# Order of an mLSTM head's products: the first output gate tile goes between the keys and the values

## The chip, the cores and the metric

The kernel runs on one core of a Trainium2 chip. Its metric is the device time of one execution in microseconds, the median of several runs. A core has TensorE (PE, matrix products into PSUM banks), VectorE (DVE), ScalarE (ACT), GpSimd (POOL) and SyncE (SP), which issues most of the DMAs. Each engine takes its instructions in order and waits for the others by semaphores.

## What is computed

Two layers of an encoder on one sequence of 512 tokens with 1024 channels, all in fp32. The sub-layer around the change is the mixer, and of it the bidirectional mLSTM branch with 4 heads of 256 channels. Cut to what matters:

```python
z = u @ w_in
qk_m, v_m, o_m, gate_m, qkv_a, gates_br = split(z)
def mlstm_branch(qk, v, o_pre, gate_pre, ...):
    qk = silu(centred_dwconv(qk, conv_w, conv_b))     # width 5
    q, k = split(qk); q = heads(q) * 256 ** -0.5
    h = mlstm_scan(q, k, v, i_f, f_f) + flip(mlstm_scan(flip(q), flip(k), flip(v), ...))
    hn = (h - mean(h)) * rsqrt(var(h) + eps)          # over a head's channels
    return sigmoid(o_pre) * hn * gn_w
# mlstm_scan: num = (q k^T * decay) v, den = its row sum, h = num / max(|den|, exp(-m))
```

## The kernel before

Every product of two fp32 matrices is done as three: each operand is split into a high half, rounded to fp32r (a cast on ACT, L87), and a low half, the rest (a subtraction on DVE, L88), and `mm3` issues high·high, low·high and high·low (L91 to L93). Weights come from HBM by SP's queue in loads of 1 MB into two raw buffers; each load is split in two parts into a ring of two pairs of high and low tiles, so the split of a third part waits until the products of the first have been done.

The mLSTM stage of a layer has for each head these blocks of products with the input u (8 slices of 128 channels), in `head_gemm`: two tiles each of queries and keys (`head_qk`, tiles `qk`, 24 products of 512 columns each); the values in two halves of 256 tokens (`head_v`, tiles `mv`, two of 128 tokens in each half, 48 products of 256 columns a half); two tiles of the output gate (`head_o`, tiles `o`, 24 products each). A half of the values goes over its first weights (`wvh`, `wvl`) for the first 12 products of a tile, and over the second from the 13th. A key tile is copied out of PSUM by ACT (`zp`, L1077), goes through the convolution (`cy`: L1079 on ACT, four L1081 on DVE), a tanh on ACT (L1082) and a product on DVE (L1083), and is split (`qkh`). A value tile is split out of PSUM (`vh` on ACT, L1105, `vl` on DVE, L1106). A gate tile goes through a tanh on ACT (`so`, L1114) and a scaling in place (L1116).

Then `head_scores` makes the weights `pt` of the numerator (it begins with `Amx`, L1144), and `head_out` does for each of four blocks of 128 tokens a numerator (`num`, 15 products a direction pair) and an output: `ht` is num over den (L1193 on ACT, L1194 on DVE), then its normalisation, its transposes on PE (`htp`, L1208) and its product with `so` (L1210, DVE).

What sets the order is `weave`: it takes one step of `head_gemm` for head h+1, then one step of `head_out` for head h. Each `yield` ends a step: a tile of queries, keys or gate, or a half of the values. The steps of `head_out` follow the table `HO`: numerators 0 and 1, output 0, numerator 2, output 1, numerator 3, outputs 2 and 3. Instructions of each engine stand in the order in which the code issues them, apart from small shifts by the builder (two numerator products, say, stand ahead of the block they belong to). Head 0's gate and queries are done elsewhere (`begun`), so a layer has three heads with the whole sequence.

PSUM tiles come in rings of two banks with a tag: "g" for queries, keys, gate tiles and the first half of the values; "A" for the second half of the values, numerators 1 and 3 and `Amx`; "n" for numerators 0 and 2; "S" for `htp` and the scores. A tile waits for the readers of the one that had its bank before.

Of the kernel before, what the change touches and what calls it, by code (L numbers as in the profile page):

```python
# [65 lines left out]
def encoder(ctx: ExitStack, tc: tile.TileContext, a, depth):  # L66
# [13 lines left out]
    def ps_tile(tag, name, shape=(P, T)):  # L80
        return psum.tile(list(shape), F32, tag=tag, name=name)
# [4 lines left out]
    def split(hi, lo, src, eng=None):  # L86
        S.copy(hi, src)  # L87
        (eng or V).tensor_tensor(lo, src, hi.bitcast(F32), op=ALU.subtract)  # L88

    def mm3(out, lh, ll, rh, rl, first, last):  # L90
        mm(out, lh, rh, start=first, stop=False)  # L91
        mm(out, lh, rl, start=False, stop=False)  # L92
        mm(out, ll, rh, start=False, stop=last)  # L93
# [24 lines left out]
    def w_feature(src, ktiles, name, own=None, count=2, eng=None):  # L118


        n = src.shape[1]
        cols = 2048 // ktiles
        srcv = src.rearrange("(k p) n -> p k n", p=P)
        for c0 in range(0, n, cols):
            cw = min(cols, n - c0)
            raw = raw_tile(name)
            rv = raw[:, :ktiles * cw].rearrange("p (k n) -> p k n", k=ktiles)
            Y.dma_start(rv, srcv[:, :, c0:c0 + cw])
            for j in range(cw // P):
                r = rv[:, :, j * P:(j + 1) * P]  # L130
                if own is not None and c0 // P + j < count:
                    yield split_own(r, ktiles, own, eng)
                    continue
                wh, wl = w_pair(name, 0, ktiles, P)
                split(wh, wl, r, G if name in POOL else V)
                yield [wh[:, k, :] for k in range(ktiles)], [wl[:, k, :] for k in range(ktiles)]
# [11 lines left out]
    def w_token(src, c0, cw, ktiles, name, own=None, own_k=(), early=False):  # L148

        srcv = src.rearrange("(k p) n -> p k n", p=P)  # L150
        per_raw = 2048 // cw
        per = 1024 // cw
        cuts = list(range(0, ktiles, per_raw)) + [ktiles]
        raws = []

        def load():
            i = len(raws)
            if i + 1 < len(cuts):
                k0, k1 = cuts[i], cuts[i + 1]
                raw = raw_tile(name)  # L160
                raws.append(raw[:, :(k1 - k0) * cw].rearrange("p (k n) -> p k n", n=cw))
                Y.dma_start(raws[i], srcv[:, k0:k1, c0:c0 + cw])

        if early:
            load()
        for i, (k0, k1) in enumerate(zip(cuts, cuts[1:])):
            load()
            rv = raws[i]
            for j in range(0, k1 - k0, per):
                m = min(per, k1 - k0 - j)  # L170
                if k0 + j in own_k:
                    for h in range(m):
                        wh, wl = own(), own()
                        split(wh[:], wl[:], rv[:, j + h, :])
                        yield wh[:], wl[:]
                else:
                    wh, wl = w_pair(name, SH if cw == 256 else 0, per, cw)
                    split(wh[:, :m], wl[:, :m], rv[:, j:j + m, :])
                    for h in range(m):
                        yield wh[:, h, :], wl[:, h, :]  # L180
# [554 lines left out]
    for l in range(depth):  # L735
# [13 lines left out]
        def slot(name, dt=F32):  # L749
            return X.tile([P, T], dt, tag="q", name=name, bufs=Q)  # L750
# [5 lines left out]
        def wk(name, shape=(P, T)):  # L756
            r = roles[name]
            return YP.tile(list(shape), F32, tag=r, name=name, bufs=depths[r])
# [303 lines left out]
        def product(w, name, fine):  # L1062

            if fine:
                return (yield from gemm_steps(w, uk, KT, name))
            return gemm_f(w, uk, KT, name)

        def head_qk(h, sec, out, fine=False):

            src = w_in[:, sec * COL_K + h * 256:sec * COL_K + h * 256 + 256]  # L1070
            for d, w in enumerate(w_feature(src, KT, "wqk")):
                n = sec * 8 + 2 * h + d
                ps = yield from product(w, "qk", fine)
                zp = wk("zp", (P, T + 4))
                G.memset(zp[:, 0:2], 0.0)
                G.memset(zp[:, T + 2:T + 4], 0.0)
                S.copy(zp[:, 2:T + 2], ps[:])  # L1077
                y = wk("cy")
                S.activation(y[:], zp[:, 0:T], AF.Identity, bias=vec["convb"](n), scale=vec["conv"](0, n))  # L1079
                for j in range(1, 5):  # L1080
                    V.scalar_tensor_tensor(y[:], zp[:, j:j + T], vec["conv"](j, n), y[:], op0=ALU.mult, op1=ALU.add)  # L1081
                S.activation(zp[:, 0:T], y[:], AF.Tanh, scale=0.5)  # L1082
                V.scalar_tensor_tensor(y[:], zp[:, 0:T], 1.0, y[:], op0=ALU.add, op1=ALU.mult)  # L1083
                th, tl = slot("qkh", F32R), slot("qkl", F32R)
                split(th[:], tl[:], y[:], G if n % 2 in GQ else V)
                out.append((th, tl))
                yield

        def head_v(h, out):
            vh = YP.tile([P, 4, NVP], F32R, tag="v", name="vh", bufs=VB)  # L1090
            vl = YP.tile([P, 4, NVP], F32R, tag="v", name="vl", bufs=VB)
            G.memset(vh[:, :, 256:257].bitcast(F32), 1.0)
            G.memset(vh[:, :, 257:258].bitcast(F32), 0.0)
            G.memset(vl[:, :, 256:258].bitcast(F32), 0.0)
            ws = list(w_token(w_in, COL_V + h * 256, 256, KT, "wv"))
            for i0 in (0, 2):
                pss = [ps_tile(MV[i0 // 2], "mv") for _ in range(2)]
                for k0 in (0, 4):
                    for i, ps in zip((i0, i0 + 1), pss):
                        for kk in range(k0, k0 + 4):  # L1100
                            uh, ul = uk[kk]
                            mm3(ps[:, 0:256], uh[:, i * P:(i + 1) * P], ul[:, i * P:(i + 1) * P],
                                ws[kk][0], ws[kk][1], kk == 0, kk == KT - 1)
                for i, ps in zip((i0, i0 + 1), pss):
                    S.copy(vh[:, i, 0:256], ps[:, 0:256])  # L1105
                    V.tensor_tensor(vl[:, i, 0:256], ps[:, 0:256], vh[:, i, 0:256].bitcast(F32), op=ALU.subtract)  # L1106
                yield
            out.extend((vh, vl))

        def head_o(h, out, fine=False):  # L1110
            so = X.tile([P, 2, T], F32, tag="hg", name=f"so{h}", bufs=4)
            for d, w in enumerate(w_feature(w_in[:, COL_O + h * 256:COL_O + h * 256 + 256], KT, "wo")):
                ps = yield from product(w, "o", fine)
                S.activation(so[:, d, :], ps[:], AF.Tanh, scale=0.5)  # L1114
                gn = vec["gnh"][:, 2 * h + d:2 * h + d + 1]
                S.activation(so[:, d, :], so[:, d, :], AF.Identity, bias=gn, scale=gn)  # L1116
                yield
            out.append(so)
# [8 lines left out]
        def head_gemm(h, out, begun=()):  # L1127

            so, qk = begun or ([], [])
            vs, o = [], [so]  # L1130
            if not begun:
                yield from head_qk(h, 0, qk)
            yield from head_qk(h, 1, qk)
            yield from head_v(h, vs)
            if not begun:
                o = []
                yield from head_o(h, o)
            out.extend((qk, *vs, o[0]))

        def head_scores(h, qk):  # L1140
# [89 lines left out]
        for _ in head_gemm(0, hd, lead):  # L1230
            pass
        for h in range(MH):
            qk, vh, vl, so = hd
            hgt.append(so)
            side = head_out(h, *head_scores(h, qk), vh, vl, so)
            if h < MH - 1:
                hd = []
                weave(head_gemm(h + 1, hd), side, *WV)
# [190 lines left out]
```

## Time and profile before

| | |
|---|---|
| median of 3 runs | 2280.37 us (2280.28 to 2283.35) |
| the profiled execution | 2288.52 us |
| its span, first to last instruction | 2286.7 us |
| PE busy | 2201.6 us, 96% of the span |
| PE's weight loads | 80% |
| DVE, ACT, POOL busy | 58%, 39%, 14% |
| mean granted PE clock | 0.985 |

All times of rows are from the profiled execution. A row of a timeline has the start in us from the span's start, the duration, the engine, the line of the kernel, the operation, output<-inputs and shapes; brackets at its end tell how long the engine idled before it and which instruction released it. PE's products overlap: the distance from one start to the next is what one of them costs.

### The profile page before, as it was taken

What the parts mean: (1) busy time and instruction counts of PE and PEld (TensorE: products, weight loads), DVE (VectorE), ACT (ScalarE), POOL (GpSimd) and SP (SyncE); (2) the same over time, 40 slices, a digit from 0 to 9 for tenths busy, and PEclk for the clock granted to TensorE, in tenths of its full rate; (3) what the DMA queues carried; (4) which work ended last, traced back from release to release, by engine and by line L of the source; (5) the groups of instructions that cost most, each with busy time, mean ns of one, the idle gap of its engine ahead of it and who ended that gap; (6) DMA issues with size and microseconds to landing.
All of it is one profiled execution on the core that took longest, in us unless ns stands there. A gap on an engine that the chain in (4) does not pass through costs nothing.

```text
span 2286.7 us, 30972 instructions
## 1 busy us (share of the span) xinstructions
PE 2201.6 (96%) x12353; PEld 1836.4 (80%) x12353; DVE 1315.9 (58%) x2242; ACT 884.0 (39%) x1465; POOL 321.6 (14%) x318
## 2 busy tenths in 40 slices
PE   6999999999999999999989999999999999999998
PEld 5878877878888878788878788788888879788886
DVE  8655458778554766564654544577764454633346
ACT  3544345544333522222354443455543324223222
POOL 4100013222000240000040000233300022200001
PEclk8999999999999999999999999999999999999999
DMA  8523322232343466554543223112212344423334
GB/s 239 186 83 107 101 66 97 74 111 80 111 157 113 155 206 205 189 193 167 189 152 98 61 92 107 56 62 69 74 56 92 111 157 157 152 83 102 100 112 157
DMA packets 244064, 278.79 MB, mean 122 GB/s; under 512 B 10280, under 2 KB 191184, under 8 KB 243920
## 3 DMA queue, kind: packets, MB, share of 16 engines
q1 hardware_dynamic: 238848, 258.97, 35.1%
q0 software_dynamic: 3584, 12.58, 1.6%
q10 hardware_dynamic: 1488, 5.26, 0.6%
q8 instruction: 97, 1.59, 0.3%
q14 instruction: 47, 0.39, 0.1%
HBM read 264.18 MB, written 12.60 MB: 121 GB/s over the span
## 4 chain that ended last, share of the span: by engine, by line
PE 75%; DVE 14%; ACT 3%; issue 3%; DMA 3%; POOL 2%; POOLq 0%; DVEq 0%; ACTq 0%; SPq 0%
PE z L93 6%; PE z L92 6%; PE z L91 6%; DVE cy L1081 4%; DMA aw<-in_w_ada 2%; PE aq L91 2%; PE ak L91 2%; PE f1y L92 2%; PE av L91 2%; PE f1y L91 2%; PE f1y L93 2%; PE av L93 2%; PE av L92 2%; PE aq L93 2%; PE aq L92 2%
## 5 line engine op out<-in xcount | busy, mean ns | idle before, releaser
L283 DVE SCALAR_TENSOR_TENSOR acc<-aw,cact,acc 128x512 f32<-128x512 f32 x140 | 118.3, 845 | 49.8 <-DMA aw<-in_w_ada 47.6
L1081 DVE SCALAR_TENSOR_TENSOR cy<-zp,vcols,cy 128x512 f32<-128x512 f32 x128 | 115.6, 903 | 10.4 <-ACT cy L1079 8.5
L87 ACT CAST w3h<-w 128x1024 fp32r<-128x1024 f32 x40 | 42.1, 1053 | 157.3 <-PE z L92 153.2
L88 POOL TENSOR_TENSOR wqkl<-wqk,wqkh 128x1024 fp32r<-128x1024 f32 x32 | 78.0, 2438 | 161.4 <-ACT wqkh L87 159.5
L978 ACT ACTIVATE xs<-xs,sm 128x512 f32<-128x512 f32 x64 | 46.2, 723 | 133.3 <-DVE sm L977 129.6
L87 ACT CAST w1h<-w 128x1024 fp32r<-128x1024 f32 x40 | 42.0, 1050 | 139.9 <-PE z L92 134.9
L88 DVE TENSOR_TENSOR w1l<-w,w1h 128x1024 fp32r<-128x1024 f32 x40 | 49.4, 1234 | 77.3 <-ACT w1h L87 77.3
L1337 DVE TENSOR_TENSOR sl<-sl,z 128x512 f32<-128x512 f32 x44 | 30.2, 687 | 104.9 <-PE z L93 101.2
L976 DVE CUSTOM_DVE_ANT_0 xs<-sc,bias 128x512 f32<-128x512 f32 x64 | 43.9, 691 | 74.7 <-PE sc L970 63.7
L91 PE MATMUL z<-um0h,w3h 128*128 128x512 f32 x160 | 64.2, 401 | 4.0 <-DVE sl L1337 4.0
L91 PE MATMUL z<-um1h,w3h 128*128 128x512 f32 x160 | 63.5, 397 | 1.8 <-DVE sl L1337 1.8
L93 PE MATMUL z<-um1h,w3l 128*128 128x512 f32 x160 | 63.6, 398 | 1.0 <-DVE w3l L88 1.0
L93 PE MATMUL z<-um0h,w3l 128*128 128x512 f32 x160 | 63.9, 400 | 0.5 <-DVE w3l L88 0.5
L92 PE MATMUL z<-um0l,w3h 128*128 128x512 f32 x160 | 63.8, 399 | 0.0
L92 PE MATMUL z<-um1l,w3h 128*128 128x512 f32 x160 | 63.2, 395 | 0.0
L91 PE MATMUL z<-um0h,w1h 128*128 128x512 f32 x160 | 63.1, 394 | 0.0
L93 PE MATMUL z<-um0h,w1l 128*128 128x512 f32 x160 | 62.7, 392 | 0.0
L92 PE MATMUL z<-um0l,w1h 128*128 128x512 f32 x160 | 62.5, 391 | 0.0
L91 PE MATMUL z<-um1h,w1h 128*128 128x512 f32 x160 | 62.4, 390 | 0.0
L93 PE MATMUL z<-um1h,w1l 128*128 128x512 f32 x160 | 62.3, 390 | 0.0
L92 PE MATMUL z<-um1l,w1h 128*128 128x512 f32 x160 | 62.2, 389 | 0.0
L935 POOL DMA_DIRECT2D vrow<-nat x16 | 11.8, 736 | 345.0 <-ACT nat L928 344.9
(544 smaller groups left out, 7268.0 us busy)
## 6 DMA issues: line engine op xcount, KB each, us to landing
w<-in_w SPq DMA_DIRECT2D x44, 1024.0 KB
aw<-in_w_ada SPq DMA_DIRECT2D x160, 256.0 KB
wqk<-in_w_in SPq DMA_DIRECT2D x16, 1024.0 KB
wav<-in_w_in SPq DMA_DIRECT2D x12, 1024.0 KB
wak<-in_w_in SPq DMA_DIRECT2D x20, 512.0 KB
f0v<-in_w SPq DMA_DIRECT2D x10, 1024.0 KB
f1v<-in_w SPq DMA_DIRECT2D x10, 1024.0 KB
waq<-in_w_in SPq DMA_DIRECT2D x18, 512.0 KB
```

The costliest lines, as they stand in the source:

```text
L87: S.copy(hi, src)
L88: (eng or V).tensor_tensor(lo, src, hi.bitcast(F32), op=ALU.subtract)
L91: mm(out, lh, rh, start=first, stop=False)
L92: mm(out, lh, rl, start=False, stop=False)
L93: mm(out, ll, rh, start=False, stop=last)
L283: V.scalar_tensor_tensor(acc[:], raws[k][:], c, acc[:], op0=ALU.mult, op1=ALU.add)
L935: G.dma_start(rows[i0 * P:(i0 + 2) * P, :].rearrange("(i p) c -> p i c", p=P), nat[:])
L976: V.tensor_tensor_reduce(x[:], sc[:], bias_tile(ti), 1.0, -3e38, ALU.add, ALU.max, sm[:, 0:1])
L978: S.activation(x[:], x[:], AF.Exp, bias=sm[:, 1:2], scale=ch, accum_out=sm[:, 2:3])
L1081: V.scalar_tensor_tensor(y[:], zp[:, j:j + T], vec["conv"](j, n), y[:], op0=ALU.mult, op1=ALU.add)
L1337: V.tensor_tensor(t[:], t[:], p3[:], op=ALU.mult)
```

## The change

In heads 1 to 3 the first tile of the output gate is now computed between the second tile of the keys and the first half of the values; the second gate tile stays behind the values. `head_o` becomes a generator that is advanced by one step there and run to its end later.

```diff
             vs, o = [], [so]
             if not begun:
+                o = []
+                outputs = head_o(h, o)
                 yield from head_qk(h, 0, qk)
             yield from head_qk(h, 1, qk)
+            if not begun:
+                yield next(outputs)
             yield from head_v(h, vs)
             if not begun:
-                o = []
-                yield from head_o(h, o)
+                yield from outputs
             out.extend((qk, *vs, o[0]))
```

With the table of steps, the products of head h+1 (left) and the steps of head h (right, num and out) alternate as follows. Before: q0 num0, q1 num1, k0 out0, k1 num2, v0 out1, v1 num3, o0 out2, o1 out3. After: q0 num0, q1 num1, k0 out0, k1 num2, **o0** out1, v0 num3, v1 out2, o1 out3. Lines behind the change are three higher in the kernel after (L1193 becomes L1196, L1208 becomes L1211); L1114 and L1116 are not.

ACT in head 1 of layer 0, before, from the second key tile's L1079 (zp_3897, cy_3901) on; mv are the four value tiles, wo the raw gate weights:

```order
L1079 ACTIVATE cy_3901<-zp_3897,vcols_688 128x512 [waits Activation_49,Pool_49]
L87 CAST qkh_3857<-cy_3849 128x512 [waits DVE_49]
L1193 ACTIVATE ht_3938<-num_3913,dn_3930 128x256 [waits DVE_49,PE_49]
L1082 ACTIVATE zp_3897<-cy_3901 128x512 [waits DVE_49,Activation_49]
L1105 CAST vh_3947<-mv_3962 128x256 [waits PE_49]
L87 CAST qkh_3909<-cy_3901 128x512 [waits DVE_49]
L1105 CAST vh_3947<-mv_3963 128x256 [waits PE_49]
L87 CAST woh_4111<-wo_4109 128x1024 [waits DMAHW7_49,PE_49]
L1105 CAST vh_3947<-mv_4020 128x256 [waits PE_49]
L1105 CAST vh_3947<-mv_4021 128x256 [waits PE_49]
```

ACT at the same place after (wvh_3997 is the cast of the values' second weights, so1 the gate):

```order
L1079 ACTIVATE cy_3901<-zp_3897,vcols_688 128x512 [waits Activation_49,Pool_49]
L87 CAST qkh_3857<-cy_3849 128x512 [waits DVE_49]
L1196 ACTIVATE ht_3938<-num_3913,dn_3930 128x256 [waits DVE_49,PE_49]
L1082 ACTIVATE zp_3897<-cy_3901 128x512 [waits DVE_49,Activation_49]
L87 CAST wvh_3997<-wv_3991 128x1024 [waits PE_49]
L87 CAST qkh_3909<-cy_3901 128x512 [waits DVE_49]
L1114 ACTIVATE so1_3947<-o_3954 128x512 [waits PE_49]
L1116 ACTIVATE so1_3947<-so1_3947,gnh_696 128x512 [waits Activation_49]
L1105 CAST vh_3986<-mv_4001 128x256 [waits PE_49]
L1105 CAST vh_3986<-mv_4002 128x256 [waits PE_49]
L1196 ACTIVATE ht_4080<-num_4055,dn_4072 128x256 [waits DVE_49,PE_49]
```

The casts of the gate weights (woh) left this stretch, since o0 has been computed by then; in their place the second cast of the value weights and the tanh and scaling of o0 stand behind L1082 of the second key tile.

PE in the first half of the values, before, at the second tile (mv_3963): the first weights are wvh_3954, and the wait is for ACT.

```order
L93 MATMUL mv_3962<-wvh_3954,u0l_105 128x256
L91 MATMUL mv_3962<-wvh_3954,u0h_104 128x256
L92 MATMUL mv_3962<-wvl_3955,u0h_104 128x256
L93 MATMUL mv_3962<-wvh_3954,u0l_105 128x256
L91 MATMUL mv_3963<-wvh_3954,u0h_104 128x256 [waits Activation_49]
L92 MATMUL mv_3963<-wvl_3955,u0h_104 128x256
```

PE in the first half of the values after (first weights wvh_3993, second wvh_3997; num_4055 is numerator 3 of head 0):

```order
L91 MATMUL mv_4001<-wvh_3993,u0h_104 128x256
L92 MATMUL mv_4001<-wvl_3994,u0h_104 128x256
L93 MATMUL mv_4001<-wvh_3993,u0l_105 128x256
L91 MATMUL mv_4001<-wvh_3997,u0h_104 128x256 [waits Activation_49]
L91 MATMUL num_4055<-vh_3436,pt_3567 128x258 [waits PE_49]
L92 MATMUL num_4055<-vl_3437,pt_3567 128x258
L91 MATMUL mv_4002<-wvh_3993,u0h_104 128x256 [waits Activation_49]
L92 MATMUL mv_4002<-wvl_3994,u0h_104 128x256
```

The 13th product of the first value tile, over the second weights, now waits for ACT, and the second value tile (mv_4002) waits for ACT behind it; two numerator products stand between them.

PE after, at the end of that numerator and the start of the second half of the values (mv_4089):

```order
L93 MATMUL num_4055<-vh_3436,pt_3568 128x258
L91 MATMUL num_4056<-vh_3436,pt_3569 128x258 [waits PE_49]
L92 MATMUL num_4056<-vl_3437,pt_3569 128x258
L93 MATMUL num_4056<-vh_3436,pt_3570 128x258
L1211 MATMUL htp_4143<-ident_66,ht_3938 128x128 [waits PE_49]
L1211 MATMUL htp_4143<-ident_66,ht_3938 128x128
L91 MATMUL mv_4089<-wvh_3993,u0h_104 128x256 [waits Activation_49]
L92 MATMUL mv_4089<-wvl_3994,u0h_104 128x256
```

The numerator now stands ahead of the second half of the values, whose first tile waits for ACT; before, that half stood ahead of the numerator.

## Rows read from the trace of the kernel before

**Rows 1.** The page: span, busy time of the engines, chain by engine.

```profile
span 2286.7 us, 30972 instructions
...
PE 2201.6 (96%) x12353; PEld 1836.4 (80%) x12353; DVE 1315.9 (58%) x2242; ACT 884.0 (39%) x1465; POOL 321.6 (14%) x318
...
PE 75%; DVE 14%; ACT 3%; issue 3%; DMA 3%; POOL 2%; POOLq 0%; DVEq 0%; ACTq 0%; SPq 0%
```

**Rows 2.** Timeline of PE, head 1 of layer 0 (start us, duration, ...).

```profile
409.80 0.28 PE L91 MATMUL mv<-wvh,u0h 128*128 128x256 f32 x1
...
412.76 0.38 PE L91 MATMUL mv<-wvh,u0h 128*128 128x256 f32 x1 [1.39 <-ACT zp L1077]
...
417.11 0.36 PE L91 MATMUL mv<-wvh,u0h 128*128 128x256 f32 x1
...
423.50 0.39 PE L91 MATMUL num<-vh,pt 128*128 128x258 f32 x1 [0.50 <-DVE vl L1106]
...
425.41 0.39 PE L91 MATMUL o<-u0h,woh 128*128 128x512 f32 x1
...
430.88 0.38 PE L1208 MATMUL htp<-ident,ht 128*128 128x128 f32 x2
...
436.73 0.71 PE L1144 MATMUL Amx<-mhl,sel 128*128 128x512 f32 x2
```

**Rows 3.** Timeline of PE, layer 1: last head's values, two Amx.

```profile
1625.90 0.71 PE L1144 MATMUL Amx<-mhl,sel 128*128 128x512 f32 x2
...
1662.64 0.38 PE L91 MATMUL mv<-wvh,uf0h 128*128 128x256 f32 x1 [1.37 <-ACT zp L1077]
...
1686.62 0.72 PE L1144 MATMUL Amx<-mhl,sel 128*128 128x512 f32 x2
```

**Rows 4.** Timeline of ACT, head 1 of layer 0.

```profile
417.78 0.64 ACT L1082 ACTIVATE zp<-cy 128x512 f32<-128x512 f32 x1 [0.23 <-DVE cy L1081]
...
418.32 0.35 ACT L1105 CAST vh<-mv 128x256 fp32r<-128x256 f32 x1
...
419.18 0.62 ACT L87 CAST qkh<-cy 128x512 fp32r<-128x512 f32 x1 [0.50 <-DVE cy L1083]
...
423.31 1.05 ACT L87 CAST woh<-wo 128x1024 fp32r<-128x1024 f32 x1
...
426.45 0.48 ACT L1193 ACTIVATE ht<-num,dn 128x256 f32<-128x256 f32 x1 [2.08 <-DVE dn L1191]
```

**Rows 5.** Timeline of DVE, head 1 of layer 0: convolution of the second keys.

```profile
413.65 0.75 DVE L1081 SCALAR_TENSOR_TENSOR cy<-zp,vcols,cy 128x512 f32<-128x512 f32 x1 [0.27 <-ACT cy L1079]
```

**Rows 6.** The gate tiles: xcount: min/median/max ns, first to last start.

```profile
L1114 ACT ACTIVATE so<-o x16: 576/592/595, 317.8 to 1687.0; 128x512 f32<-128x512 f32 x16
```

**Rows 7.** Timeline of PE, head 2 of layer 0.

```profile
478.30 0.38 PE L92 MATMUL mv<-wvl,u0h 128*128 128x256 f32 x1 [2.95 <-DVE wvl L88]
...
488.85 0.39 PE L91 MATMUL num<-vh,pt 128*128 128x258 f32 x1 [1.89 <-DVE vl L1106]
...
491.03 0.63 PE L91 MATMUL o<-u0h,woh 128*128 128x512 f32 x1
...
497.80 0.38 PE L1208 MATMUL htp<-ident,ht 128*128 128x128 f32 x2
```

**Rows 8.** PE by windows (us, busy, granted clock, DMA, GB/s), and a row of PE's timeline.

```profile
413.00:414.00 1.00, 1.00 (x10) 1.00 0.28 52
...
480.00:481.00 1.00, 1.00 (x11) 1.00 1.05 361
...
491.00:492.00 1.00, 1.00 (x5) 0.50 0.48 115
...
366.42 0.39 PE L92 MATMUL mv<-wvl,u0h 128*128 128x256 f32 x1 [2.66 <-DVE wvl L88]
```

**Rows 9.** Timelines of SP's queue and ACT: a load and its reader.

```profile
2262.20 0.37 SPq L162 DMA_DIRECT2D f1v<-in_w  x1
...
2267.23 1.05 ACT L87 CAST f1vh<-f1v 128x1024 fp32r<-128x1024 f32 x1 [2.56 <-DMA f1v<-in_w]
```

## The prediction

> **What bounds the kernel now.** I read the page's busy shares first. TensorE (PE) is busy for 2201.6 of 2286.7 us, VectorE (DVE) for 58%, and 75% of the chain that ended last is PE's [rows 1]. So a new order can give back only moments in which PE idles, and it costs what it adds to them. The change touches heads 1 to 3 of each layer's mLSTM stage, six places. Next I read PE's timeline through one of them, head 1 of layer 0 [rows 2]. The reader is to see two idle moments in brackets: 1.39 us at 412.76, where the 13th value product needs the PSUM bank that ScalarE's (ACT) copy of the second key tile (zp, L1077) frees, and 0.50 us at 423.50, where the numerator needs the low halves of the values (vl, L1106). The rest of these 27 us runs back to back. Five of the six heads show this pair, first [rows 2] and last [rows 3]; head 2 of layer 0 waits 2.95 and 1.89 us instead [rows 7].
>
> So the two existing waits, 1.89 us in a head, are all that the change can take away there. In the new order the first goes: the first gate tile (o0) now stands between the keys and the values, and runs over the copy. The second goes too, since a whole block of values lies between a vl and its reader.
>
> **The change part by part.** *Work.* Nothing is added or removed: the same products, casts and copies in another order, so the cost is the difference in idle time. I walk the new order of PE and ACT with the durations of before, from the same start, 409.80, since all up to there stands in the old order.
>
> o0 is 24 products, 425.41 to 430.88, 5.47 us, and a pair of transposes (htp) takes 0.13 [rows 2]. The values then start at 409.80 + 5.47 + 0.13 = 415.40. A block of 48 value products takes 423.50 − 0.50 − 417.11 = 5.89 us, 0.123 each, so the first 12 are through at 416.87.
>
> *First new wait.* The 13th reads the second half of the cast value weights (wvh). Its slot is that of o0's second weights, so the cast can't start before o0's end, 415.27; before, those weights were already there. On ACT it stands behind L1082 of the second key tile. That one started at 417.78, after DVE's L1081, and ACT went on at 418.32 [rows 4]. This is DVE's chain of the convolution, which began at 413.65 [rows 5]; nothing in the change stands before it, so I leave its times. A cast of this size takes 1.05 us [rows 4]: 418.32 + 1.05 = 419.37, and PE idles 419.37 − 416.87 = 2.50 us. Queued behind the waiting product on PE are two numerator products and all of the values; ACT's later casts of values wait for PE in turn. Bounds: 2.3 if ACT passes its queue a little sooner, 2.9 with a hop of some tenths at each hand-over, as the 0.23 and 0.50 of [rows 4].
>
> *Second new wait.* After the 13th and two numerator products (0.37 together) PE is at 419.74. The second value tile takes o0's PSUM bank, which the tanh (L1114) must read first. On ACT that stands behind the key's cast (qkh), 0.62 us [rows 4], starting near 419.27, then 0.59 of its own [rows 6]: 420.38, each starting 0.1 before the printed end of its neighbour, as 418.32 does. Idle: 0.64. Bounds 0.4 and 1.0.
>
> *Third new wait.* 35 value products (4.30) and 13 of the numerator (at 1.91/15 = 0.127: 1.65) end at 426.33; the transposes follow to 426.46. The second half of the values takes the banks of that numerator, which were free before it ran in the old order. Their reader is ACT's ht (L1193), then DVE. Before, the numerator ended at 425.41 and ht at 426.45 + 0.48 = 426.93, 1.52 us later [rows 2, 4]. So the next block starts at 427.85, idle 1.39. DVE's part frees the second bank within the 1.47 us of 12 products. Bounds 0.9 and 1.6.
>
> *Behind it.* The second block (48 products), o1 and the next head's scores follow as before, and o1's tanh has as much room as the old one had. Sum: 2.50 + 0.64 + 1.39 − 1.89 = +2.64 us in a head, 2.3 + 0.4 + 0.9 − 1.89 = 1.7 to 2.9 + 1.0 + 1.6 − 1.89 = 3.6 by the bounds.
>
> *Head 2 of layer 0.* Its key chain on DVE is mixed with other work, and its waits are 4.84 already [rows 7], so the new ones partly fall on the old ones. Bounds 0 and 2.64; I take the middle, 1.3. Five heads at 2.64 and this one: 14.5 us; by the bounds 8.5 to 20.6.
>
> *Loads.* The raw value weights are split some 9 us later, and the next queries' load takes over their buffer from SyncE's (SP) queue; the keys' load does so with the gate weights, some 8 us later. A load of 1 MB went from issue at 2262.20 to its first reader at 2267.23, 5.03 us [rows 9]; the next head reads its queries over 10 us after that buffer is free. I cost it at nothing: the values and o1 cover it. If this cover were gone, the price is at most those 5 us a head. The last head's gate weights are followed by another load in the same way, at most 0.5 us in each layer, which I leave out of the sum.
>
> *Clock.* PE's granted clock stood at 1.00 behind the 1.39 wait, at full 2.4 GHz (413 to 414), and at 0.50, 1.2 GHz, from 491 on, behind the 1.89 wait [rows 8]. Waits of 2.66 and 2.95 lie in this stage too [rows 7, 8]; the latter was not followed at once by a fall, at 480 the clock was 1.00 [rows 8]. What a fall costs: o0 started at 491.03 and ended at 497.80, 6.77 against 5.47, 1.3 more [rows 2, 7]; the numerator ahead of it took 491.03 − 488.85 = 2.18 against 1.91, 0.3 more. I take 1.5 us. The new first wait, 2.50, is nearest to the 1.89 and the 2.66 and not to the 1.39, and two more waits follow in ten microseconds, so I charge one fall to each of the five heads: 7.5 us. Head 2 has its fall already. Bounds: none, or a second fall in each.
>
> *Sum.* 14.5 + 7.5 = +22.0 us. The profiled execution took 2288.52 us (span 2286.7), which would be 2310.5; the median of the runs is 8.15 lower, 2280.37. The same 22.0 on it gives 2302.4.
>
> **The rivals.** *A, the clock stays.* PE waits as worked out, but the low clock comes in none of the five heads. For it: 2.95 with no fall at once. Against it: 1.89 and 2.66 with one. Time: +14.5, 2294.9, with the bounds 2289 to 2301.
>
> *B, faster.* The copy of the second key is covered by o0, and nothing takes its place: ACT would have to cast wvh before PE wants it at 416.87, and do the tanh before the second value tile. Then the old pairs go, 5 × 1.89 = 9.5, and up to 4.84 in head 2: 2266, or, where the third new wait stays (1.39 in a head), 5 × 0.50 and up to 3.4: 2274. It is decided on ACT by the place of wvh behind L1082: if the first two new waits together stay under 1.89 − 1.39 = 0.50 us, a head is no slower than before. The 417.78 of [rows 4] speaks against it, nearly a microsecond too late before the cast even starts. The Trainium skill, in "Perfetto Trace Analysis", section "Optimizing Tensor Performance", says that independent groups of products should rotate through PSUM banks so that ACT and DVE empty one while the next is computed; by that rule alone the change is a gain, as in this rival, for it parts the keys from the values by a group in another bank. The trace agrees on the bank that is freed, but the new waits are on a weight slot and on banks of other tiles.
>
> *C, no change.* The new waits come to the old sum, 1.9 in a head. With the third at 1.39 the first two must shrink from 3.14 to 0.50, so the convolution on DVE would have to end 2.6 us sooner; its time is 2276 to 2285.
>
> *D, still slower.* A second fall in each head, or a load that isn't hidden: another 7.5 to 10, 2310 to 2313.
>
> **How the numbers follow.** Forecast (waits and one fall in most heads): 0.60. A: 0.21. D: 0.07. B: 0.06. C: 0.06. The predicted time is 2302. The range takes the forecast's and A's bounds, from 2289 (8.5 us of waits) to 2312 (22.0 plus a size error or second falls in some heads of nearly 10); it leaves out B, C and some of D. A difference under 0.2%, 4.6 us, is about what a measurement can't tell from no change. Slower by more than that: 0.60 + 0.21 + 0.07 = 0.88; within it 0.06; faster 0.06.
>
> **What the profile after would show.** In each of the six heads: no wait on zp L1077 or vl L1106; a wait of about 2.5 on ACT's cast of wvh at the 13th value product, 0.6 on the tanh of so, and 1.4 on ACT's ht ahead of the second half of the values. From one Amx to the next in layer 1, 1686.62 − 1625.90 = 60.72 now [rows 3], I expect 63.4 without a fall of the clock and 64.9 with one, and some three slices of a microsecond near 0.50 behind the first wait. Wrong would be: the first wait below 1 us (ACT came to the cast sooner, rival B or C), no low clock (A), a wait on a load (D), or a stretch of DVE's convolution that moved, since every anchor of the first two waits is its end.

## The result, and the profile after

The changed kernel takes 2307.9 us (median of four runs, 2302.68 to 2308.87). The kernel before takes 2280.32 over its four runs beside it, and 2281.52 and 2281.28 over the 11 and the 23 runs beside the experiments. The ratio is 1.0114, with an interval from 1.0098 to 1.013. That is some 26 us more (22 to 30 by the interval), where 22 were forecast; 2307.9 lies in the range.

The page of the profile after shows little of this, as the change adds no work; the lines answer to [rows 1]:

```profile
span 2307.0 us, 30959 instructions
...
PE 2206.7 (96%) x12353; PEld 1840.4 (80%) x12353; DVE 1319.4 (57%) x2242; ACT 883.1 (38%) x1465; POOL 322.2 (14%) x318
```

PE's busy time has grown by 5 us with the same products, and by 10 us within the six heads that changed: there the same instructions are longer, since the clock is low in a part of them (below). The rest is idle time. PE's timeline of head 1 of layer 0, which answers to [rows 2]:

```profile
419.48 0.58 PE L91 MATMUL mv<-wvh,u0h 128*128 128x256 f32 x1 [2.34 <-ACT wvh L87]
...
429.03 0.39 PE L91 MATMUL mv<-wvh,u0h 128*128 128x256 f32 x1 [1.48 <-ACT ht L1196]
...
440.19 0.71 PE L1147 MATMUL Amx<-mhl,sel 128*128 128x512 f32 x2
```

The reader is to see that the two old waits (on zp L1077 and on vl L1106) are gone, and two others, of 2.34 and 1.48 us, have come. Their causes stand in ACT's timeline of the same place, which answers to [rows 4]:

```profile
417.86 0.63 ACT L1082 ACTIVATE zp<-cy 128x512 f32<-128x512 f32 x1 [0.24 <-DVE cy L1081]
...
418.40 1.03 ACT L87 CAST wvh<-wv 128x1024 fp32r<-128x1024 f32 x1
...
419.33 0.61 ACT L87 CAST qkh<-cy 128x512 fp32r<-128x512 f32 x1
...
419.85 0.59 ACT L1114 ACTIVATE so<-o 128x512 f32<-128x512 f32 x1
...
428.50 0.47 ACT L1196 ACTIVATE ht<-num,dn 128x256 f32<-128x256 f32 x1 [2.33 <-DVE dn L1194]
```

L1082 of the second key tile waits for DVE's taps until 417.86, as before (417.78). The cast of the second value weights follows at 418.40 and ends at 419.43, and PE goes on at 419.48. Behind the cast stand the key's cast and the gate's tanh, the second new wait. In this head it doesn't show, since PE was slow at that point; in layer 1 it does. From one Amx to the next in layer 1, with the three new waits between, to be held against the wait and the two Amx of [rows 3], which are the next head's:

```profile
1579.79 0.71 PE L1147 MATMUL Amx<-mhl,sel 128*128 128x512 f32 x2
...
1623.46 0.38 PE L91 MATMUL mv<-wvh,uf0h 128*128 128x256 f32 x1 [2.62 <-ACT wvh L87]
...
1624.47 0.58 PE L91 MATMUL mv<-wvh,uf0h 128*128 128x256 f32 x1 [0.39 <-ACT so L1114]
...
1630.00 0.28 PE L93 MATMUL num<-vh,pt 128*128 128x258 f32 x1
...
1633.44 0.38 PE L91 MATMUL mv<-wvh,uf0h 128*128 128x256 f32 x1 [1.48 <-ACT ht L1196]
...
1644.59 0.71 PE L1147 MATMUL Amx<-mhl,sel 128*128 128x512 f32 x2
```

1644.59 − 1579.79 = 64.80 us, where this head took 60.69 before (and the next one, of [rows 3], 60.72). The clock, in windows of PE (us, busy, granted clock, DMA, GB/s), head 1 of layer 0 first, then head 2 of layer 0, then the head of layer 1 just shown:

```profile
418.00:419.00 1.00, 0.00 (x0) 1.00 0.00 0
...
420.00:421.00 1.00, 1.00 (x5) 0.50 0.00 0
...
423.00:424.00 1.00, 1.00 (x11) 1.00 0.25 38
...
430.00:431.00 1.00, 1.00 (x11) 1.00 0.00 0
...
489.00:490.00 1.00, 1.00 (x5) 0.50 0.00 0
...
493.00:494.00 1.00, 1.00 (x7) 0.50 1.09 387
...
1625.00:1626.00 1.00, 1.00 (x7) 0.50 0.00 0
```

In head 1 the clock is at 1.00 (2.4 GHz) in the wait itself but for its end, at 0.50 (1.2 GHz) behind it, and at 1.00 again from 423 on; behind the third wait, which ended at 429.03, nothing fell. In head 2 the fall came within the wait, and the clock was low from before 489 to beyond 494, about twice as long. PE and ACT there:

```profile
488.43 0.58 PE L91 MATMUL mv<-wvh,u0h 128*128 128x256 f32 x1 [5.05 <-ACT wvh L87]
...
510.60 0.71 PE L1147 MATMUL Amx<-mhl,sel 128*128 128x512 f32 x2
...
486.45 0.63 ACT L1082 ACTIVATE zp<-cy 128x512 f32<-128x512 f32 x1 [2.78 <-DVE dn L1192]
...
487.34 1.03 ACT L87 CAST wvh<-wv 128x1024 fp32r<-128x1024 f32 x1
```

The six heads, from the first Amx of one head's scores to the next head's, in the two profiled executions, and what the difference is made of (us); the last column is what the waits over 0.3 us don't account for:

| head | before | after | difference | new waits less old | rest |
|---|---|---|---|---|---|
| layer 0, 1 | 60.50 | 63.83 | +3.33 | 1.93 | 1.40 |
| layer 0, 2 | 66.90 | 70.41 | +3.51 | 1.69 | 1.82 |
| layer 0, 3 | 61.13 | 65.51 | +4.38 | 2.36 | 2.02 |
| layer 1, 1 | 60.40 | 64.37 | +3.97 | 2.31 | 1.66 |
| layer 1, 2 | 60.69 | 64.80 | +4.11 | 2.62 | 1.49 |
| layer 1, 3 | 60.72 | 64.66 | +3.94 | 2.28 | 1.66 |

Together +23.2 us: 13.2 of waits and 10.0 of rest. The rest is the low clock, or nearly all of it: in each head it is, to within 0.1 us, what PE is busy longer with the same products (60.31 us for 58.82 in the second head of layer 1), and the granted clock over a head fell from 1.00 to 0.97, in head 2 of layer 0 from 0.97 to 0.95. The two profiled executions as wholes differ by less, 20.3 us (2308.84 and 2288.52), since the one of before was 2.9 us longer outside of these heads. That part took between 1906 and 1916 us over the traces of all kernels here, the 1916 in the kernel before. So the distance from 23.2 to 26 lies within what executions of one kernel differ by (the kernel before ran between 2275.9 and 2288.5, its profiled execution included).

### The profile page after: what moved, and what is told of

The parts are those of the page before. It is cut to its first block, busy times and chain, and to the rows that moved or that the text cites. A ratio compares the mean times of both kernels' runs of the same rounds, so it can differ in the third digit from the quotient of the medians.

```text
span 2307.0 us, 30959 instructions
## 1 busy us (share of the span) xinstructions
PE 2206.7 (96%) x12353; PEld 1840.4 (80%) x12353; DVE 1319.4 (57%) x2242; ACT 883.1 (38%) x1465; POOL 322.2 (14%) x318
## 4 chain that ended last, share of the span: by engine, by line
PE 73%; DVE 14%; DMA 4%; ACT 4%; issue 3%; POOL 2%; POOLq 0%; DVEq 0%; SPq 0%; ACTq 0%
PE z L93 6%; PE z L92 6%; PE z L91 6%; DVE cy L1081 4%; DMA aw<-in_w_ada 2%; PE aq L91 2%; PE ak L91 2%; PE f1y L92 2%; PE f1y L91 2%; PE f1y L93 2%; PE ak L93 2%; PE ak L92 2%; PE aq L93 2%; PE aq L92 2%; PE mv L91 1%
```

## The experiments

My theory had two halves: each new wait can be placed beforehand, on ACT's queue or in a PSUM bank, and the first of them also costs a stretch at the low clock. The rivals were that the new waits would be paid later anyway, that the weight slot or a load and not ACT's queue makes the first wait, and that the convolution chain sets the pace of the stage whatever PE waits for.

### One wait alone: the second half of the values in another ring

```diff
-MV = 'gA'
+MV = 'gn'
```

> The kernel after, with the second half of the values in PSUM ring n instead of A, so that it no longer takes the banks of the numerator ahead of it. My account (three new waits in a head, one of them, 1.48 us, on the ht that empties these banks): the third wait goes in all six heads, the others stay, 8 to 9 us less than the kernel after, about 2298. Rival (the time of the change is the late weight split alone and the third wait would be paid anyway a little later): within 3 us of the kernel after.

2295.53 us, ratio to before 1.0061 (1.0048 to 1.0075), 12 us less than the kernel after. PE in layer 1, second head, with one window of its clock:

```profile
1567.76 0.71 PE L1147 MATMUL Amx<-mhl,sel 128*128 128x512 f32 x2
...
1611.42 0.39 PE L91 MATMUL mv<-wvh,uf0h 128*128 128x256 f32 x1 [2.62 <-ACT wvh L87]
...
1612.43 0.38 PE L91 MATMUL mv<-wvh,uf0h 128*128 128x256 f32 x1 [0.38 <-ACT so L1114]
...
1614.65 0.39 PE L92 MATMUL mv<-wvl,uf0h 128*128 128x256 f32 x1 [0.54 <-DVE wvl L88]
...
1630.25 0.71 PE L1147 MATMUL Amx<-mhl,sel 128*128 128x512 f32 x2
...
1613.00:1614.00 1.00, 1.00 (x10) 1.00 0.00 0
```

The wait on ht is gone in all six heads, which together take 9.45 us less than in the kernel after. This head takes 1630.25 − 1567.76 = 62.49 us against 64.80, the two others of layer 1 1.9 and 1.6 less. Its 2.31 are not the wait of 1.48 alone: behind the wait of 2.62 the clock stayed at 1.00 here, where it fell in the five other heads of this run, so that PE is busy for 58.95 us and not for 60.31; and a wait of 0.54 on wvl, the low half of the cast weights, shows instead. The account of the third wait holds; in the medians the gain is a little more than the 8 to 9 expected. The head without a fall also tells the price of one: it takes 1.80 us more than before (60.69), its waits over 0.3 us are 1.67 more, and 0.13 is left as rest, where the kernel after has 1.49.

### The clock: the first two waits filled with products

```diff
                 for k0 in (0, 4):
                     for i, ps in zip((i0, i0 + 1), pss):
+                        if fill and i == 1 and k0 == 0:
+                            pf = ps_tile("S", "fill")
+                            for n in range(fill):
+                                mm(pf[:], uk[n % KT][0][:, 0:P], uk[n % KT][0][:], ...)
```

with `fill` at 15 in heads 1 to 3.

> The kernel after with 15 extra products of 512 columns (nothing reads them) at the place of the first two new waits in heads 1 to 3; work is added that no output needs. It takes 3.5 us in a head, the waits it covers are 2.34 and up to 0.7. My account (the low clock follows the wait, and costs about 1.5 us in a head): granted clock near 1.00 behind the products in five heads, a head 0.5 to 1.2 us shorter than after, 3 to 8 us less in all. Rival (the fall comes of something else than the wait, or costs nothing, since PE waits for others at that time): the extra 0.4 to 0.6 us in a head is lost, and the time is 2 to 4 us more than after.

2304.09 us, ratio to before 1.0099 (1.0083 to 1.0114): by the medians 3.8 us less than the kernel after, although 15 × 6 products that nothing reads were added (the two intervals overlap, so the gain is not certain; the 2 to 4 us more of the rival did not come). The same head, PE and its windows:

```profile
1573.42 0.72 PE L1151 MATMUL Amx<-mhl,sel 128*128 128x512 f32 x2
...
1620.35 0.38 PE L92 MATMUL mv<-wvl,uf0h 128*128 128x256 f32 x1 [0.46 <-DVE wvl L88]
...
1637.93 0.48 PE L1151 MATMUL Amx<-mhl,sel 128*128 128x512 f32 x1
...
1616.00:1617.00 1.00, 1.00 (x6) 1.00 0.00 0
...
1622.00:1623.00 1.00, 1.00 (x11) 1.00 1.01 333
```

The clock stays at 1.00 through the filled stretch and behind it, in five heads; in head 2, whose wait is longer than the filling, PE still waits 2.69 and the clock falls. The head takes 1637.93 − 1573.42 = 64.51 us against 64.80. The filling is 3.5 us long, up to where the tanh would be done anyway, then PE still waits 0.46 for wvl, and 15 numerator products instead of 13 are left: so of the stretch at the low clock, about 1.2 us by this head's products (in the kernel after, 35 of the values from 1624.47 to 1630.00, 5.53 us, instead of 35 × 0.123 = 4.30), 0.3 are left as a gain. I had expected 0.5 to 1.2 us a head; only heads 2 and 3 of layer 0 gain that much (0.55 and 0.80), those of layer 1 gain 0.2 to 0.4, and head 1 of layer 0 loses 0.2. So where the waits are filled there is no fall. Its price isn't read from this run but from the products and from the head without a fall above.

### Both old waits taken out of the kernel before

```diff
-MV = 'gA'
+MV = 'Ag'
```

in the order of before.

> The kernel before, in its own order of products, with the two halves of the values in each other's PSUM ring: the first half in A, the second in g. The first half's second tile then needs a bank that numerator 1's ht left long ago, the numerator a bank whose vl is done. My account (the waits of before are waits for banks): both old waits, 1.39 and 0.50, go in five heads and part of 4.84 in head 2: 9 to 14 us less than before, about 2269. Rival (the convolution chain on DVE and ACT sets the pace, so that a wait taken away comes back at the scores): within 4 us of before.

2271.72 us, ratio 0.9957 (0.9944 to 0.9969), some 10 us less than before. PE in layer 1:

```profile
1551.96 0.72 PE L1144 MATMUL Amx<-mhl,sel 128*128 128x512 f32 x2
...
1599.46 0.50 PE L91 MATMUL o<-uf0h,woh 128*128 128x512 f32 x1 [0.33 <-DVE vl L1106]
...
1610.87 0.71 PE L1144 MATMUL Amx<-mhl,sel 128*128 128x512 f32 x2
```

Neither zp nor vl ahead of the numerator is waited for; a wait of 0.33 on vl ahead of the gate tile is new, since that tile now takes a bank of the values. A head takes 1610.87 − 1551.96 = 58.91 against 60.69, 1.78 less, close to the 1.87 that its two waits were worth; the other heads take 1.7 to 2.0 less. So what the change takes away was worth taking, and there is a way to it without any move. "Perfetto Trace Analysis" of the Trainium skill, section "Optimizing Tensor Performance", asks for groups of products to rotate through banks so that one is emptied under the next; here this run agrees, with 1.78 us in a head.

### Both gate tiles ahead of the values

```diff
             if not begun:
-                yield next(outputs)
+                yield from outputs
             yield from head_v(h, vs)
-            if not begun:
-                yield from outputs
```

with the halves of the values in rings n and g:

> Both gate tiles between the keys and the values, the first half of the values in ring n and the second in g. Then o1 stands over the second key tile's L1082, the weight splits have a whole tile of time, and no half of the values takes a bank that is still read. My account: none of the three new waits and none of the old ones but part of head 2's, 9 to 16 us less than before, 2264 to 2271, no low clock in these heads. Rival (a gate tile ahead of the values delays the loads or the values' low halves until the next scores): new waits at the scores or on raw loads, within 5 us of before or slower.

2268.22 us, ratio 0.9943 (0.9928 to 0.9957), the fastest of all. Rows of PE (two Amx of layer 1, the wait left of the old ones in head 2 of layer 0, and a new one in head 3 of layer 0):

```profile
1550.49 0.72 PE L1145 MATMUL Amx<-mhl,sel 128*128 128x512 f32 x2
...
1608.48 0.72 PE L1145 MATMUL Amx<-mhl,sel 128*128 128x512 f32 x2
...
482.89 0.39 PE L92 MATMUL mv<-wvl,u0h 128*128 128x256 f32 x1 [1.03 <-DVE wvl L88]
...
536.15 0.65 PE L293 MATMUL adaps<-ident,acc 128*128 128x128 f32 x4 [1.93 <-ACT ht L1194]
```

1608.48 − 1550.49 = 57.99 us in a head, 2.70 less than before: no wait over 0.3 us is left between these two (1.87), and PE is busy 0.83 less (58.82 before). The second gate tile is 5.5 us of work under which ACT passes the second key tile and does the weight casts. One thing that I had expected failed: in head 3 of layer 0 products of another block (adaps, L293) now wait 1.93 us for ht, the clock falls behind that (0.97 over the head), and this head takes 1.1 us more than before.

With the rings as before (g and A):

> Both gate tiles between the keys and the values, with the halves of the values in rings g and A as before. It tells the order from the banks. My account: the new waits of the change are gone here too, since the casts have o1's time, and the numerator stands a whole half ahead; but the second half holds the banks that the next head's Amx takes, so 1.0 to 1.5 us ahead of Amx in each head, on vl: 6 to 9 us more than both_gates_ahead, about 2275. Rival (the order alone gives the gain): within 3 us of both_gates_ahead.

2268.80 us, ratio 0.9939 (0.9927 to 0.9951), level with the other rings. Here my account fell. I had charged 1.0 to 1.5 us ahead of each Amx for banks that the values still hold:

```profile
1554.43 0.48 PE L1145 MATMUL Amx<-mhl,sel 128*128 128x512 f32 x1
...
1555.67 0.39 PE L1145 MATMUL Amx<-mhl,sel 128*128 128x512 f32 x1
...
1612.43 0.48 PE L1145 MATMUL Amx<-mhl,sel 128*128 128x512 f32 x1
```

1612.43 − 1554.43 = 58.00 us: the second Amx now comes 1.24 us behind the first, and products of the scores fill the time between, since the builder put them there. The order alone gives the gain, and the wait of 1.93 in head 3 of layer 0 is there with these rings too.

### What makes the first wait: ACT's queue or the weight slot

Everything between L1079 and the split is left out for the second key tile of heads 1 to 3, in the kernel after and in the kernel before:

```diff
-                for j in range(1, 5):
-                    V.scalar_tensor_tensor(y[:], zp[:, j:j + T], vec["conv"](j, n), y[:], ...)
-                S.activation(zp[:, 0:T], y[:], AF.Tanh, scale=0.5)
-                V.scalar_tensor_tensor(y[:], zp[:, 0:T], 1.0, y[:], ...)
+                if not (h and sec and d):
+                    ...
```

> The kernel after, but for the second key tile of heads 1 to 3 everything behind L1079 is left out up to the split: the four taps of the convolution on DVE, the tanh on ACT and the product on DVE, so the output is another. My account (the first two new waits are ACT's queue: the weight cast and the gate's tanh stand behind that tile's tanh, which waits for DVE's taps): the cast comes right behind o0's end, both waits shrink to 0.3 us or less in all, no low clock behind them, the third wait, 1.48, stays; 20 to 28 us less than after, 2280 to 2288. Rival (the weight slot, freed by o0's end only, or the raw load sets the first wait): it stays above 1.5 us in each head and the time falls by less than 10.

> The kernel before with the same work left out for the second key tile of heads 1 to 3, so the output is another: what leaving it out gives by itself. Neither of the old waits hangs on this tile's taps (zp L1077 stands ahead of them, vl behind). My account: the waits on zp stay near 1.4 and the time is within 6 us of before, mostly from head 2; then after_no_key_chain is level with it or up to 5 us slower, and the order of the products costs little without that chain. Rival (the chain holds up the whole stage, not the new waits): 15 us or more less than before, and after_no_key_chain as far above it as after is above before.

The kernel after falls to 2283.26 us, ratio 1.0010 (0.9999 to 1.0021); the kernel before to 2276.38, ratio 0.9975 (0.9967 to 0.9984). So the same work left out is worth 25 us to the one and 5 to the other, and the price of the order falls from 26 to 7 us. PE in layer 1, first of the kernel after without the chain, with ACT's second cast of the value weights as its last row, then of the kernel before without it:

```profile
1561.33 0.72 PE L1148 MATMUL Amx<-mhl,sel 128*128 128x512 f32 x2
...
1602.19 0.35 PE L91 MATMUL mv<-wvh,uf0h 128*128 128x256 f32 x1
...
1604.55 0.39 PE L92 MATMUL mv<-wvl,uf0h 128*128 128x256 f32 x1 [0.60 <-DVE wvl L88]
...
1611.04 0.39 PE L91 MATMUL mv<-wvh,uf0h 128*128 128x256 f32 x1 [1.48 <-ACT ht L1197]
...
1622.38 0.71 PE L1148 MATMUL Amx<-mhl,sel 128*128 128x512 f32 x2
...
1600.55 1.05 ACT L87 CAST wvh<-wv 128x1024 fp32r<-128x1024 f32 x1 [0.19 <-PE o L92]
```

```profile
1557.09 0.72 PE L1145 MATMUL Amx<-mhl,sel 128*128 128x512 f32 x2
...
1593.84 0.39 PE L91 MATMUL mv<-wvh,uf0h 128*128 128x256 f32 x1 [1.36 <-ACT zp L1077]
...
1617.15 0.71 PE L1145 MATMUL Amx<-mhl,sel 128*128 128x512 f32 x2
```

In the first the waits on wvh and on the tanh are gone in five heads, and the granted clock over these heads is 1.00. The slot is still freed only at o0's end, and now the cast starts right there, at 1600.55, and is through at 1601.60, before the first 12 value products are (1602.19). So it wasn't the slot. One thing else changed: the builder let 12 products of the second value tile go ahead of the 13th of the first. The answer doesn't rest on that, since the cast is done before those 12 begin. In head 2 of layer 0 a wait of 2.34 on the tanh stays, with a fall of the clock; there the cast starts only at 479.55, behind ACT's instructions for the first key tile, which was left as it is. What is left in the five heads is 0.60 to 0.66 on wvl, the subtraction behind the cast, which I hadn't counted: hence 7 us where I had 0 to 5. The head takes 61.05 instead of 64.80 us. In the second the 1.36 on zp stays and the 0.50 on vl is gone, which I had wrong too: I took vl for free of the key's chain. The likely link is DVE, which had the chain's taps ahead of vl; it was not followed further.

### The change in layer 1 alone

```diff
-            if not begun:
+            if not begun and l == 1:
                 yield next(outputs)
```

> The change in layer 1 alone. My account (each of the six places pays for itself): layer 1's three heads take 4.0 us more each, layer 0's as before, 11 to 15 us more than before, about 2294. Rival (part of the loss comes later, from loads that start late, or from one layer alone): under 8 or over 19 us.

2290.54 us, ratio 1.0039 (1.0026 to 1.0051), 9 us more than before, less than the 11 to 15 expected. In the trace layer 1's heads are 64.36, 64.90 and 64.68 us long, 12.1 more than before, as in the kernel after. So each of these places pays for itself; the shortfall is elsewhere. Head 2 of layer 0, which has the old order here, also differs from the execution shown before:

```profile
435.53 0.71 PE L1147 MATMUL Amx<-mhl,sel 128*128 128x512 f32 x2
...
487.65 0.39 PE L91 MATMUL num<-vh,pt 128*128 128x258 f32 x1 [0.32 <-DVE vl L1106]
...
500.87 0.71 PE L1147 MATMUL Amx<-mhl,sel 128*128 128x512 f32 x2
```

Its second wait is 0.32, not 1.89 as in [rows 7], and the head takes 500.87 − 435.53 = 65.34 instead of 66.90. The order is the same in both, so this is a difference of 1.6 us between two executions, and it does not explain a difference of medians. Outside of the six heads the two differ by more, 1906.1 us here and 1916.4 before, so that their spans are nearly level (2286.9 and 2286.7). The interval of the medians (5.9 to 11.6) ends a little under the 12.1 of the heads; where the remainder went is not shown.

## Why the prediction was right, point by point

- **The old waits go:** right, in all six heads.
- **First new wait:** 2.50 forecast, 2.33 to 2.62 measured in five heads, on the cast that was named, and for the cause that was named: without the key's chain it is gone in these five.
- **Second new wait:** 0.64 forecast, 0.39 or 0.40 in four heads and none in two, heads 1 and 2 of layer 0. In these two the clock fell within the first wait (in the others only behind it), so PE's three products up to the second wait were slower, and it was covered.
- **Third new wait:** 1.39 forecast, 1.48 to 1.51 measured; taken out by another ring, it was gone for good.
- **Clock:** one fall in each of five heads was forecast at 1.5 us; the rest column gives 1.40 to 1.66 in four of them and 2.02 in head 3 of layer 0, where 35 value products took 5.90 us and not 5.53; why was not followed further. Rival A (no fall) is out, since the clock fell in all six heads. That it fell in all of them is partly luck: with the other ring it didn't fall behind one of these very waits.
- **Head 2 of layer 0:** the term that was mis-sized: +3.5 measured, +1.3 forecast. Of it, 1.69 is waits, within my bounds of 0 to 2.64, but not by the thought behind them, that new waits would fall on old ones. The key's chain didn't get shorter: from the first product behind the keys to L1082 it took 10.67 us in both (472.29 to 482.96 before, 475.78 to 486.45 after), and the wait on wvh became 5.05. The other 1.82 is the low clock, which I had put at nothing since the head has its fall already; behind the longer wait the low stretch became about twice as long.
- **Loads:** no wait of PE over 0.3 us on one, as forecast (rival D).
- **Rival B** was decided where the prediction put it, by the 417.8 of L1082. With both gate tiles ahead that point is passed during o1, and the gain comes, 13 us.
- **The sum:** 22.0 forecast, 23.2 in the heads and 26 in the medians. In the heads the waits are 13.2 us where 14.5 were forecast, the rest 10.0 where 7.5 were charged for the clock: two errors of opposite sign, which partly cancel in the sum. Head 2 alone is 2.2 over, the five others together 1.0 under. The distance to the medians isn't explained further than by the spread of executions.

## What to carry to other kernels

When a block of products is moved, walk its helpers in order on every engine, not only the wait that it is meant to cover: here the block brought its weight split and its eviction forward, behind an instruction on ACT that waits for DVE. Look first for the bank or slot that makes an old wait; swapping two rings took the two old waits out in five heads with no move. And moving two blocks can gain where moving one of them loses, as the second gives the first one's helpers their time.

## What the runs showed of the hardware

In the kernel after the clock fell behind the first wait in all six heads (waits of 2.33 to 5.05 us), and behind none of the third waits (1.48 to 1.51). But the length of a wait alone does not decide it. With the second half of the values in ring n it fell in five heads and stayed at 1.00 behind the wait of 2.62 in the sixth; in the kernel before it did not fall at once behind 2.95, and fell behind 1.89 [rows 8].

Nor does the length of the wait alone give the length of the low stretch. In the kernel after that was about twice as long behind the wait of 5.05 (low from before 489 to beyond 494) as behind that of 2.34 in head 1; but with the other ring it was low from 549 to beyond 555 behind a wait of 2.34 in head 3 of layer 0. With useless products in the place of the first two waits the clock fell in none of the five heads that they covered, and the kernel was by the medians 3.8 us faster, a gain that the intervals leave uncertain.
